# Places of the projections' operands in memory, and a last norm without a second spread

## The chip, the cores and the metric

The kernel runs on one core of a Trainium2 chip. The metric is the device time of one execution in microseconds, median over several runs. Five engines work side by side and wait for one another through semaphores: PE (TensorE, matrix products into PSUM), ACT (ScalarE), DVE (VectorE), POOL (GpSimd) and SP (SyncE, which here issues most DMAs). On-chip memory (SBUF) has 128 partitions; a tile occupies the same bytes in each of them. PE reads its operands from SBUF and writes to PSUM.

## The reference

One inference step of a small encoder trunk, float32, width 2048, for 256 frames of a new stream and 32 frames of a running one. The kernel puts both side by side: T = 288 columns. With `rmsnorm(x, g) = x * rsqrt(mean(x*x) + 1e-6) * g`:

```python
for l in range(2):
    h = rmsnorm(x, norm_mix_g[l])
    mix = ab_mixer(h) if l == 0 else c_mixer(h)   # retention and GLA heads; band attention
    x = x + mix                                   # both end in a projection 2048 -> 2048
    h = rmsnorm(x, norm_ffn_g[l])
    g, u = split(h @ w_up)                        # 2048 -> 2 * 5632
    act = silu(conv3(g) + b) * u
    x = x + act @ w_down                          # 5632 -> 2048
y = rmsnorm(x, norm_final_g)
```

States of the heads, keys and values and the last rows of the convolution are outputs too. All weights are float32 and each is used once.

## The kernel before

Everything lies with features on partitions: a tile [128, 288] holds 128 features of all tokens, and x is 16 of them. A projection makes one output tile [128, 288] in a PSUM bank by summing over k-tiles of 128 input features (`project`, lines 61 to 74). A float32 product is made of float32r ones (rounded operands, which PE takes in one pass): each operand is split into a rounded part and the rest, h and l, and three products are summed, h·xh, h·xl and l·xh (`passes`, lines 77 to 81). So each k-tile costs three matmuls of 288 columns, each with its own load of 128 x 128 weights.

Weights come in tiles of up to 8 k-tiles (`weights`, lines 50 to 59): SP issues the DMA into w (4 buffers), ACT casts it into wh, DVE makes wl (3 buffers each). The moving operands are of two kinds. xh and xl, 16 tiles each, hold the split x with a norm's gain (`gain_in`, lines 135 to 141); they feed the input projection, q, k, v and the FFN's up projections, and the norm's factor R is multiplied in behind them. bh and bl hold what goes into output and down projections: 16 tiles each in a pool of their own, and for the FFN six more, bh16 to bh21 and bl16 to bl21, which `ffn` takes from its pool. The FFN is done in two halves of 22 hidden tiles: 22 pairs of up projections, then 16 down projections over the 22 k-tiles of that half, added to x.

The order of each engine's work is the order in which the program issues it; a tile framework adds the waits. Tiles of a pool lie one behind another in the order in which they are first asked for, each rounded up to 32 bytes, and a pool opened later begins where the one before ends. The first pool, "const", holds xh0 to xh15, xl0 to xl15, R, ones, gains and ident in this order; then come the pools of the weights, of small tiles, and the rest.

Norms: while x[m] becomes final, ACT squares it and DVE adds the squares into ssq (`square_in`). `norm_stat` (from line 156) sums ssq over partitions with the tokens as outputs (9 or 18 matmuls of one column), takes the inverse root of 3 columns on 96 partitions, and spreads it again: DVE scales an identity by it, PE multiplies that by all ones, ACT copies the result to R, [128, 288]. At the end of the last FFN the last square goes into a tile of its own (sq_last) and is a second summand. Then y = x * R, with the gain already in x but for the last tile: 11 products on DVE and 5 on POOL, stored in four DMAs of 2, 4, 5 and 5 tiles, all issued by SP.

Of the kernel before, what the change touches and what calls it, by code (L numbers as in the profile page):

```python
# [33 lines left out]
class Trunk:  # L34
# [15 lines left out]
    def weights(self, src, n, lo=False):  # L50
        """n k-tiles of 128 rows: the float32 tile as the sum of two float32r tiles."""
        nc = self.nc
        w = self.wp.tile([P, WCH, P], F32, name="w", tag="w", bufs=4)[:, :n, :]
        h = self.wp.tile([P, WCH, P], F32R, name="wh", tag="wh", bufs=3)[:, :n, :]
        l = self.wp.tile([P, WCH, P], F32R, name="wl", tag="wl", bufs=3)[:, :n, :]
        nc.sync.dma_start(w, src)
        nc.scalar.copy(h, w)  # L57
        nc.vector.tensor_tensor(l, w, h.bitcast(F32), op=ALU.subtract)  # L58
        return h, l

    def project(self, src, xh, xl, nk, k0=0, chunks=None, part=None, ps=None):
        """PSUM [128 outputs, T]: the product over nk k-tiles of float32 operands split in two."""
        if ps is None:
# [19 lines left out]
    def first_project(self, src, x):  # L83
        """As project, while the input is loaded and the first norm's operands come about."""
        nc = self.nc
# [13 lines left out]
    def first_squares(self, x):  # L99
        """The sum of squares, in the place of x."""  # L100
        nc, sq = self.nc, x
        for c in range(0, KD, 4):
            nc.scalar.activation(sq[:, c : c + 4, :], x[:, c : c + 4, :], AF.Square)
            if c:
                nc.vector.tensor_tensor(sq[:, 0:4, :], sq[:, 0:4, :], sq[:, c : c + 4, :], op=ALU.add)
        nc.vector.tensor_tensor(sq[:, 0:2, :], sq[:, 0:2, :], sq[:, 2:4, :], op=ALU.add)
        nc.vector.tensor_tensor(sq[:, 0, :], sq[:, 0, :], sq[:, 1, :], op=ALU.add)
        self.ssq = sq[:, 0, :]
# [8 lines left out]
    def rsqrt(self, out, ms_ps, inv_n, p=P, n=T, tag="rs"):  # L117
        """out = (ms_ps * inv_n + eps) ** -0.5"""
        nc = self.nc
# [10 lines left out]
    def norm_in(self, k, n):  # L130
        """x[k] is final: its split product with the gain of norm n, and its square."""
        self.gain_in(k, n)
# [23 lines left out]
    def norm_stat(self):  # L156
        """R [128, T]: each token's 1 / rms, on all partitions; worked out with tokens on partitions."""
        nc = self.nc
# [21 lines left out]
    def run(self, ctx):  # L180
# [5 lines left out]
        nc.vector.memset(self.ones, 1.0)  # L186
        self.gains = self.const("gains", [P, 5, KD], F32, a["gains"], nc.scalar)
        self.sq_last = None
# [7 lines left out]
        with self.tc.tile_pool(name="x", bufs=1) as xp:  # L196
# [5 lines left out]
            with self.tc.tile_pool(name="f0", bufs=2) as pool:  # L202
                self.ffn(pool, 0, 2)
            with self.tc.tile_pool(name="c", bufs=2) as pool:
# [5 lines left out]
            with self.tc.tile_pool(name="f1", bufs=2) as pool:  # L210
                self.ffn(pool, 1, 4)

    def chain(self, heads, front, tail):
        """Heads as generators of steps. A head's steps after its first few take turns with the next one's
        first, so that its later products find their operands ready."""
        for _ in range(front):
# [9 lines left out]
    def out_start(self, w, chunks):  # L226
        """The first halves of out_proj's first sums, which the last head is not part of."""
        self.started = [self.project(w[m], self.bh, self.bl, KD, chunks=chunks, part=0) for m in range(2)]

    def start(self, pool):  # L230
        """The first norm, and the layer's first products beside it."""
        nc, a = self.nc, self.a
# [4 lines left out]
        k0 = self.first_project(w[KB], x_in)  # L237
        # The gate's low-rank features: both parts of the weights side by side in one tile's columns
        # (their sum is taken in the product with w2, which stands twice).
        lo_ps = self.acc_ps.tile([P, 512], F32, name="acc", tag="acc")[:, :T]  # L240
# [18 lines left out]
    def out_proj(self, w, n, chunks):  # L259
        """x += o @ w, and the next norm's start."""  # L260
        for m in range(KD):
# [7 lines left out]

    def ffn(self, pool, layer, n):  # L270
        nc, a = self.nc, self.a
        convp = self._one(pool, "convp", [P, NF, 4], a["convp"][:, layer])
        hist = self._one(pool, "hist", [P, NF, 2], a["hist"][:, layer])
        conv_out = self._one(pool, "conv_out", [P, NF, 4])
        gps = [self._one(pool, f"gp{i}", [P, T + 4]) for i in range(3)]
        for gp in gps:
            nc.gpsimd.memset(gp[:, 0:2], 0.0)
        bh = self.bh + [self._one(pool, f"bh{k}", [P, T], None, F32R) for k in range(KD, HALF)]
        bl = self.bl + [self._one(pool, f"bl{k}", [P, T], None, F32R) for k in range(KD, HALF)]
        up, down = a["w_ffn_up"][layer], a["w_ffn_down"][layer]  # L280
        last = layer == 1
        for half in range(2):
# [29 lines left out]
            for m in range(KD):  # L312
                ps = self.project(down[m], bh, bl, HALF, half * HALF)
                nc.vector.tensor_tensor(self.x[m], self.x[m], ps, op=ALU.add)
                if half == 1:
                    if last:
                        self.square_in(m, m == KD - 1)
                        if m < KD - 1:
                            nc.scalar.activation(self.x[m], self.x[m], AF.Copy, scale=self.gains[:, n, m : m + 1])
                    else:  # L320
                        self.norm_in(m, n)
        self.norm_stat()
        if last:
            y = pool.tile([P, KD, T], F32, name="y", tag="y", bufs=1)
            cuts = (0, 2, 6, 11, 16)
            for i, j in zip(cuts, cuts[1:]):
                for k in range(i, j):
                    if k == KD - 1:
                        nc.vector.scalar_tensor_tensor(
                            y[:, k, :], self.x[k], self.gains[:, n, k : k + 1], self.R, op0=ALU.mult, op1=ALU.mult  # L330
                        )
                        continue
                    eng = nc.gpsimd if k % 3 == 1 else nc.vector
                    eng.tensor_tensor(y[:, k, :], self.x[k], self.R, op=ALU.mult)  # L334
                nc.sync.dma_start(a["yT"][:, i:j, :], y[:, i:j, :])

# [1 line left out]

# [5 lines left out]
    def head_out(self, pool, o, gates, hd, g):  # L344
        """Gated, normalised head output into the split operands of w_out; o: two PSUM tiles."""
        nc = self.nc
# [17 lines left out]
    def to_tokens(self, pool, feats, name, width, scale=None, bufs=1):  # L364
        """[128 tokens, 3, width] from feature-major [128, T] tiles."""
        nc = self.nc
# [21 lines left out]
    def ab_mixer(self, pool, k0, q0, lo_ps):  # L388
# [19 lines left out]
        def gates():  # L408
            """log sigmoid of the gates, tokens on partitions (its 1/16 is in the level matrices)."""
            e = pool.tile([P, 9, T], F32, name="E", tag="E").rearrange("p l t -> p (l t)")  # L410
# [38 lines left out]
    def gla_head(self, pool, hd, w, la, lvl, masks, eyem, hg, first):  # L449
# [13 lines left out]

        # E[:, l]: decays to and from the middle of each token's block of level l. Slot 7: level 256
        # (tile 0 before, tile 1 behind the middle), and from the sample's start; slot 8: to the end.
        E = pool.tile([P, 9, T], F32, name="E", tag="E", bufs=1)
# [29 lines left out]

        # Scores, transposed: each pair of tokens belongs to the one level whose middle parts them.
        pT = [pool.tile([P, T - t * P], F32, name=f"pT{t}", tag=f"pT{t}") for t in range(2)]
# [64 lines left out]

        # States.
        kf = pool.tile([P, T], F32, name="kf", tag="kf", bufs=1)
# [86 lines left out]

# [1 line left out]

    def att_head(self, pool, hd):
# [7 lines left out]
        nc.gpsimd.dma_start(vc, a["cache_v"][hd])  # L663
        # Keys stand in reversed order: the bias of query p and key column c is rel[c0 + p + c].
        bias = pool.tile([P, TP], F32, name="bias", tag="bias")
# [19 lines left out]
        nc.tensor.matmul(pss[:, TS:T], lhsT=q[:, TP:], rhs=kc, start=True, stop=True)  # L685
        # Tokens on partitions: the sample's, then the prompt's second and first 128.
        vt = pool.tile([P, 3, P], F32, name="avt", tag="avt")
# [25 lines left out]
        yield  # L713
        # Probabilities with keys on partitions: the first 128 and the second of the prompt's
        # (p0, p1), beside them the cache's two halves, and the sample's own (p2).
        p0 = pool.tile([P, T], F32, name="ap0", tag="ap0")
# [25 lines left out]
def _tiles(w):  # L742
    """[K, M] -> [M/128, 128, K/128, 128]: one output tile's rows, contiguous by partition."""
    k, m = w.shape
# [3 lines left out]
def _cols(v):  # L748
    """[..., N] -> [128, ..., N/128]: features on partitions."""
    v = v.reshape(*v.shape[:-1], v.shape[-1] // P, P)  # L750
# [110 lines left out]
```

## Time and profile before

| | us |
|---|---|
| median of 3 runs | 2762.46 (2761.59 to 2763.56) |
| the profiled execution, span from first to last instruction | 2760.1 |
| PE busy | 2732.1 |
| DVE busy | 1572.3 |
| ACT busy | 1123.9 |
| POOL busy | 126.5 |

The profile is of one execution on the one core; its own time is the span of 2760.1 us, and the timed runs hold some 2 us more around it. The page gives busy time by engine, the chain of work that ended last (at each step back to what released it), and groups of instructions by line, engine and operation with count, busy time, mean length, idle time before and what ended that. "x694: 292/294/294, 1004.8 to 1279.7" in a row of one line's instructions is their count, shortest, median and longest length in ns, and the starts of the first and the last in us.

### The profile page before, as it was taken

The page shows a single profiled execution, that of the slowest core. Times are in us where ns is not written, and L with a number is a line of the kernel's source. Part 1 is how long each engine was busy: PE and PEld are TensorE (multiplying, and loading weights), DVE is VectorE, ACT ScalarE, POOL GpSimd, SP SyncE. Part 2 cuts the span into 40 slices and gives each one's busy share as a digit, 9 for nine tenths or more (in the row PEclk, how much of TensorE's full clock was granted, in tenths as well). Part 3 has the DMA queues.
Part 4 walks back from the last instruction along what each step waited for, and adds up shares of the span by engine and source line. Part 5 has one row for each costly group of instructions (what it writes and reads, how often), then busy time and mean ns, then how long its engine had stood idle before and what let it go on. Part 6 is the DMA issues. An engine that isn't in the chain of part 4 may idle for free.

```text
span 2760.1 us, 49198 instructions
## 1 busy us (share of the span) xinstructions
PE 2732.1 (99%) x20340; PEld 2686.5 (97%) x20340; DVE 1572.3 (57%) x2536; ACT 1123.9 (41%) x1538; POOL 126.5 (5%) x440
## 2 busy tenths in 40 slices
PE   8999999999999999999999999999999999999997
PEld 7999999999999999999999999999999999999997
DVE  6566555666665456665555555556666544666544
ACT  7444343443343333334444333344333333433443
POOL 1000000000000000000011111100000000000000
PEclk9999999999999999999999999999999999999999
DMA  5334444545555555555555555544555555555553
GB/s 198 117 131 142 152 157 149 192 162 166 168 167 161 168 168 165 167 168 162 166 182 170 166 165 165 163 156 162 166 165 166 162 167 168 168 166 166 163 167 125
DMA packets 126546, 448.84 MB, mean 163 GB/s; under 512 B 15562, under 2 KB 15754, under 8 KB 126320
## 3 DMA queue, kind: packets, MB, share of 16 engines
q1 hardware_dynamic: 119520, 427.15, 48.6%
q0 software_dynamic: 6656, 18.49, 2.1%
q8 instruction: 159, 2.61, 0.4%
q14 instruction: 67, 0.55, 0.1%
q10 hardware_dynamic: 144, 0.04, 0.0%
HBM read 435.22 MB, written 10.40 MB: 161 GB/s over the span
## 4 chain that ended last, share of the span: by engine, by line
PE 97%; ACT 1%; DVE 1%; DMA 1%; issue 0%; SPq 0%; DVEq 0%; ACTq 0%
PE acc L80 31%; PE acc L79 30%; PE acc L81 30%; PE mm L520 1%; DMA x_in<-in_xT 0%; PE mm L372 0%; PE mm L643 0%; ACT wh L57 0%; PE mm L682 0%; PE mm L685 0%; PE mm L734 0%; PE mm L681 0%; DVE wl L58 0%; DVE y L334 0%; PE mm L738 0%
## 5 line engine op out<-in xcount | busy, mean ns | idle before, releaser
L57 ACT CAST wh<-w 128x1024 fp32r<-128x1024 f32 (+1 forms) x816 | 843.7, 1034 | 1505.9 <-PE acc L80 1209.0
L58 DVE TENSOR_TENSOR wl<-w,wh 128x1024 fp32r<-128x1024 f32 (+1 forms) x816 | 981.0, 1203 | 761.7 <-ACT wh L57 761.4
L79 PE MATMUL acc<-xh,wh 128*128 128x288 f32 x4480 | 1323.0, 295 | 8.6 <-ACT wh L57 7.7
L81 PE MATMUL acc<-xh,wl 128*128 128x288 f32 x4480 | 1323.5, 295 | 1.3 <-DVE wl L58 1.3
L80 PE MATMUL acc<-xl,wh 128*128 128x288 f32 x4480 | 1324.0, 296 | 0.0
L79 PEld LDWEIGHTS acc<-xh,wh 128*128 128x128 f32 x4480 | 843.2, 188 | 13.3 <-ACT wh L57 7.9
L81 PEld LDWEIGHTS acc<-xh,wl 128*128 128x128 f32 x4480 | 842.6, 188 | 2.8 <-DVE wl L58 2.1
L80 PEld LDWEIGHTS acc<-xl,wh 128*128 128x128 f32 x4480 | 843.0, 188 | 2.0 <-issue 1.0
L79 PE MATMUL acc<-bh,wh 128*128 128x288 f32 x1920 | 567.1, 296 | 0.4 <-ACT wh L57 0.4
L80 PE MATMUL acc<-bl,wh 128*128 128x288 f32 x1920 | 566.3, 295 | 0.0
L81 PE MATMUL acc<-bh,wl 128*128 128x288 f32 x1920 | 565.0, 294 | 0.0
L79 PEld LDWEIGHTS acc<-bh,wh 128*128 128x128 f32 x1920 | 360.1, 188 | 1.3 <-ACT wh L57 0.6
L81 PEld LDWEIGHTS acc<-bh,wl 128*128 128x128 f32 x1920 | 361.2, 188 | 0.0
L80 PEld LDWEIGHTS acc<-bl,wh 128*128 128x128 f32 x1920 | 360.3, 188 | 0.1
L298 DVE SCALAR_TENSOR_TENSOR gc<-gp,convp,gc 128x290 f32<-128x290 f32 x176 | 91.3, 519 | 3.2
L304 DVE TENSOR_TENSOR v<-acc,R 128x288 f32<-128x288 f32 x88 | 40.3, 458 | 87.8 <-PE acc L81 87.8
L289 DVE TENSOR_TENSOR gp<-acc,R 128x256 f32<-128x256 f32 x88 | 37.5, 426 | 88.3 <-PE acc L81 88.3
L291 POOL COPY conv_out<-gp 128x2 f32<-128x2 f32 x88 | 16.4, 187 | 1312.7 <-DVE gp L289 1312.7
L114 ACT CAST bh<-v 128x288 fp32r<-128x288 f32 x88 | 38.1, 433 | 15.3 <-DVE v L306 15.3
L296 DVE TENSOR_SCALAR gc<-gp,convp 128x290 f32<-128x290 f32 x88 | 38.0, 432 | 9.5
L305 DVE TENSOR_TENSOR v<-v,sg 128x256 f32<-128x256 f32 x88 | 37.5, 426 | 9.9 <-DVE v L304 0.9
L115 DVE TENSOR_TENSOR bl<-v,bh 128x288 fp32r<-128x288 f32 x88 | 39.8, 452 | 0.7 <-ACT bh L114 0.7
(256 smaller groups left out, 1188.2 us busy)
## 6 DMA issues: line engine op xcount, KB each, us to landing
w<-in_w_ffn_up SPq DMA_DIRECT2D x352, 512.0 KB, 3.7
w<-in_w_ffn_down SPq DMA_DIRECT2D x128, 512.0 KB, 3.7
w<-in_w_in SPq DMA_DIRECT2D x112, 512.0 KB, 3.8
w<-in_w_qkv SPq DMA_DIRECT2D x96, 512.0 KB, 3.9
w<-in_w_ffn_down SPq DMA_DIRECT2D x64, 384.0 KB, 3.2
w<-in_w_out_ab SPq DMA_DIRECT2D x32, 512.0 KB, 3.8
w<-in_w_out_att SPq DMA_DIRECT2D x32, 512.0 KB, 3.8
x<-in_xT SPq DMA_DIRECT2D x4, 576.0 KB, 6.1
```

The lines of the kernel that those rows point to most:

```text
L57: nc.scalar.copy(h, w)
L58: nc.vector.tensor_tensor(l, w, h.bitcast(F32), op=ALU.subtract)
L79: nc.tensor.matmul(ps, lhsT=h, rhs=xh, start=first, stop=False)
L80: nc.tensor.matmul(ps, lhsT=h, rhs=xl, start=False, stop=False)
L81: nc.tensor.matmul(ps, lhsT=l, rhs=xh, start=False, stop=last)
L114: self.nc.scalar.copy(h, v)
L115: self.nc.vector.tensor_tensor(l, v, h.bitcast(F32), op=ALU.subtract)
L289: nc.vector.tensor_tensor(gp[:, 2 : TP + 2], g[:, :TP], self.R[:, :TP], op=ALU.mult)
L296: nc.vector.tensor_scalar(gc, gp[:, 0:W], cw[:, 0:1], cw[:, 3:4], op0=ALU.mult, op1=ALU.add)
L298: nc.vector.scalar_tensor_tensor(gc, gp[:, w : w + W], cw[:, w : w + 1], gc, op0=ALU.mult, op1=ALU.add)
L304: nc.vector.tensor_tensor(v, u, self.R, op=ALU.mult)
L305: nc.vector.tensor_tensor(v[:, :TP], v[:, :TP], s[:, :TP], op=ALU.mult)
```

## The change

Four edits; the comments that the diff also drops are left out.

- The tile of the gains is asked for with 96 columns (384 bytes a partition) in place of 80 (320 bytes); its DMA is issued apart, as before by ACT, into the first 80.
- In `ffn`, bh16 to bh21 and bl16 to bl21 are asked for ahead of the pool's other tiles. `ffn` also takes a [128, 1] tile eps and has POOL fill it.
- In the last FFN the gain is multiplied into x[15] on ACT as well, behind its square.
- `norm_stat` is not called at the end. `out_norm` takes its place: all ones times ssq and all ones times sq_last put the sum on all partitions at once, [128, 288] in PSUM; ACT takes the square root from PSUM (scale 1/D, eps as bias), DVE makes v = sum/D + eps beside it, then the reciprocal and one Newton step, on all 288 columns. Then four products of four tiles each on DVE, with r broadcast over the four, each stored by its own DMA, issued in turn by SP and ACT.

```diff
@@ run
-        self.gains = self.const("gains", [P, 5, KD], F32, a["gains"], nc.scalar)
+        gains = self.const("gains", [P, 96])[:, : 5 * KD].rearrange("p (n k) -> p n k", n=5)
+        nc.scalar.dma_start(gains, a["gains"])
+        self.gains = gains
...
-                self.ffn(pool, 0, 2)
+                self.ffn(pool, 0, 2, x)
...
-                self.ffn(pool, 1, 4)
+                self.ffn(pool, 1, 4, x)
@@ ffn
-    def ffn(self, pool, layer, n):
+    def ffn(self, pool, layer, n, x_all):
         nc, a = self.nc, self.a
+        bh = self.bh + [self._one(pool, f"bh{k}", [P, T], None, F32R) for k in range(KD, HALF)]
+        bl = self.bl + [self._one(pool, f"bl{k}", [P, T], None, F32R) for k in range(KD, HALF)]
         convp = self._one(pool, "convp", [P, NF, 4], a["convp"][:, layer])
...
-        bh = self.bh + [self._one(pool, f"bh{k}", [P, T], None, F32R) for k in range(KD, HALF)]
-        bl = self.bl + [self._one(pool, f"bl{k}", [P, T], None, F32R) for k in range(KD, HALF)]
+        eps = self._one(pool, "eps", [P, 1])
+        nc.gpsimd.memset(eps, EPS)
...
                         self.square_in(m, m == KD - 1)
-                        if m < KD - 1:
-                            nc.scalar.activation(self.x[m], self.x[m], AF.Copy, scale=self.gains[:, n, m : m + 1])
+                        nc.scalar.activation(self.x[m], self.x[m], AF.Copy, scale=self.gains[:, n, m : m + 1])
                     else:
                         self.norm_in(m, n)
-        self.norm_stat()
         if last:
-            y = pool.tile([P, KD, T], F32, name="y", tag="y", bufs=1)
-            cuts = (0, 2, 6, 11, 16)
-            for i, j in zip(cuts, cuts[1:]):
-                for k in range(i, j):
-                    if k == KD - 1:
-                        nc.vector.scalar_tensor_tensor(
-                            y[:, k, :], self.x[k], self.gains[:, n, k : k + 1], self.R, op0=ALU.mult, op1=ALU.mult
-                        )
-                        continue
-                    eng = nc.gpsimd if k % 3 == 1 else nc.vector
-                    eng.tensor_tensor(y[:, k, :], self.x[k], self.R, op=ALU.mult)
-                nc.sync.dma_start(a["yT"][:, i:j, :], y[:, i:j, :])
+            self.out_norm(pool, x_all, eps)
+        else:
+            self.norm_stat()
+
+    def out_norm(self, pool, x, eps):
+        nc = self.nc
+        ps = self.mm()[:, :T]
+        nc.tensor.matmul(ps, lhsT=self.ones, rhs=self.ssq, start=True, stop=False)
+        nc.tensor.matmul(ps, lhsT=self.ones, rhs=self.sq_last, start=False, stop=True)
+        v = pool.tile([P, T], F32, name="fv", tag="fv", bufs=1)
+        r = pool.tile([P, T], F32, name="fr", tag="fr", bufs=1)
+        s = pool.tile([P, T], F32, name="fs", tag="fs", bufs=1)
+        nc.scalar.activation(r, ps, AF.Sqrt, bias=eps, scale=1.0 / D)
+        nc.vector.tensor_scalar(v, ps, 1.0 / D, EPS, op0=ALU.mult, op1=ALU.add)
+        nc.vector.reciprocal(r, r)
+        nc.vector.tensor_tensor(s, r, r, op=ALU.mult)
+        nc.vector.scalar_tensor_tensor(s, s, -0.5, v, op0=ALU.mult, op1=ALU.mult)
+        nc.vector.scalar_tensor_tensor(r, s, 1.5, r, op0=ALU.add, op1=ALU.mult)
+        y = pool.tile([P, KD, T], F32, name="y", tag="y", bufs=1)
+        for n, i in enumerate(range(0, KD, 4)):
+            c = slice(i, i + 4)
+            nc.vector.tensor_tensor(y[:, c, :], x[:, c, :], r[:, None, :].to_broadcast([P, 4, T]), op=ALU.mult)
+            (nc.scalar if n % 2 else nc.sync).dma_start(self.a["yT"][:, c, :], y[:, c, :])
```

## The prediction

> **What bounds the kernel now.** First the page: its busy shares, its chain of work that ended last, and its groups.
>
> ```profile
> span 2760.1 us, 49198 instructions
> ...
> PE 2732.1 (99%) x20340; PEld 2686.5 (97%) x20340; DVE 1572.3 (57%) x2536; ACT 1123.9 (41%) x1538; POOL 126.5 (5%) x440
> ...
> PEclk9999999999999999999999999999999999999999
> ...
> PE 97%; ACT 1%; DVE 1%; DMA 1%; issue 0%; SPq 0%; DVEq 0%; ACTq 0%
> ...
> L57 ACT CAST wh<-w 128x1024 fp32r<-128x1024 f32 (+1 forms) x816 | 843.7, 1034 | 1505.9 <-PE acc L80 1209.0
> ...
> L79 PE MATMUL acc<-xh,wh 128*128 128x288 f32 x4480 | 1323.0, 295 | 8.6 <-ACT wh L57 7.7
> ...
> L79 PE MATMUL acc<-bh,wh 128*128 128x288 f32 x1920 | 567.1, 296 | 0.4 <-ACT wh L57 0.4
> ```
>
> PE holds 97% of the chain at a full clock. It waits 8.6 us for weights in the whole run, while the cast of the weights waits 1209 us for PE: weights lie ready, and DMA, ACT and DVE are cover. So the time is the number of projection matmuls, (4480 + 1920) x 3 = 19200, by their step, plus the tail behind the last one. The mean of 295 ns is a pipelined length; the step comes from first and last starts. These are the rows of line 79 (one matmul of three in a k-tile) in four stretches: up projection, the two output projections, down projection.
>
> ```profile
> L79 PE MATMUL acc<-xh,wh x694: 292/294/294, 1004.8 to 1279.7; 128*128 128x288 f32 x174
> L79 PE MATMUL acc<-bh,wh x175: 295/295/297, 510.0 to 579.6; 128*128 128x288 f32 x175
> L79 PE MATMUL acc<-bh,wh x213: 295/295/297, 1809.8 to 1894.6; 128*128 128x288 f32 x107
> L79 PE MATMUL acc<-bh,wh x326: 288/295/298, 870.1 to 999.7; 128*128 128x288 f32 x163
> ```
>
> Up: 274.9 / 693 = 0.3967 us a k-tile, 132.2 ns a matmul. Output projections: 69.6 / 174 and 84.8 / 212, both 0.4000, 133.3 ns. Down: 129.6 / 325 = 0.3988, 132.9 ns. The operations are the same; what differs is where the moving operand lies. In the built program xh0 starts at byte 16512 of its partition (129 x 128) and each such tile is 1152 bytes (9 x 128), so xh and xl all start on a multiple of 128. The 320 bytes of the gains (2.5 x 128) then shift what is allocated behind them: w, wh, wl and bh0 to bh15, bl0 to bl15 stand 64 bytes past one. The small tiles of the FFN pool (convp to gp2, 5312 bytes, 41.5 x 128) shift bh16 to bh21 back onto one. The down projection thus holds the comparison inside one output: k-tiles 0 to 15 from shifted operands, 16 to 21 from unshifted ones. Its timeline, PE alone (start, length):
>
> ```profile
> 2700.34 0.29 PE L79 MATMUL acc<-bh,wh 128*128 128x288 f32 x1
> ...
> 2705.54 0.30 PE L79 MATMUL acc<-bh,wh 128*128 128x288 f32 x1
> ...
> 2705.94 0.29 PE L79 MATMUL acc<-bh,wh 128*128 128x288 f32 x1
> ...
> 2708.32 0.30 PE L79 MATMUL acc<-bh,wh 128*128 128x288 f32 x1
> ```
>
> 13 k-tiles in 5.20 us are 0.4000; the last six, from 2705.94 to the next output at 2708.32, take 2.38, 0.3967. The step changes where the operand's place changes, with the same weight buffers. A read of 1152 bytes from +64 touches ten blocks of 128 bytes, from 0 nine; the extra one would cost 1.11 ns a matmul.
>
> **The change, part one: places.** Gains take 384 bytes, and the FFN's bh16 to bl21 come first in their pool. All of wh, wl, bh, bl, xh, xl then start on multiples of 128. No instruction is added but one POOL memset for eps at each FFN's start; POOL waits at that place anyway and nothing reads eps before the end:
>
> ```profile
> L288 POOL COPY gp<-hist 128x2 f32<-128x2 f32 x88 | 17.6, 203 | 212.8 <-DVE gc L298 205.3 <-DMA hist<-in_hist 7.5
> ```
>
> If that cover were gone it would cost some 0.2 us twice. The gains' DMA stays one on ACT's queue; nothing else there moves.
>
> The moving operand: output projections 2 x 16 x 16 = 512 k-tiles x (0.4000 - 0.3967) = 1.7 us; down projections 2 x 2 x 16 x 22 = 1408 k-tiles x (0.3988 - 0.3967) = 2.9 us. Together **-4.6 us**; starts are given to 0.1 us, which leaves this between 4.0 and 5.3. The xh matmuls keep their step.
>
> The stationary operand: no row of the projections shows unshifted weights. The only weights of this size on a multiple of 128 are the all-ones tile:
>
> ```profile
> L353 PEld LDWEIGHTS mm<-hsq,ones x16: 187/188/189, 89.7 to 486.2; 128*128 128x128 f32 x16
> ...
> L79 PEld LDWEIGHTS acc<-xh,wh x694: 188/188/188, 1005.1 to 1280.0; 128*128 128x128 f32 x174
> ```
>
> Load times are alike, and a load runs beside the matmul before it, so I take 0. The bounds: 512 bytes from +64 touch five blocks, not four; at 1.11 ns each, 19200 x 1.11 = 21.3 us of gain on one side, and a loss of the same step on the other (rival A).
>
> [...]
>
> **Part two: the tail.** Before, from the last projection's sum on, every engine:
>
> ```profile
> 2743.61 0.46 DVE L314 TENSOR_TENSOR x<-x,acc 128x288 f32<-128x288 f32 x1 [6.71 <-PE acc L81]
> 2744.10 0.44 ACT L147 ACTIVATE sql<-x 128x288 f32<-128x288 f32 x1 [7.65 <-DVE x L314]
> ...
> 2744.59 0.33 PE L164 MATMUL mm<-ones,sql 128*96 128x1 f32 x2 [0.94 <-ACT sql L147]
> ...
> 2745.64 0.16 DVE L123 TENSOR_SCALAR rv<-mm 96x3 f32<-96x3 f32 x1 [1.58 <-PE mm L164]
> ...
> 2748.12 0.40 ACT L178 COPY R<-mm 128x288 f32<-128x288 f32 x1 [2.08 <-PE mm L175]
> 2748.55 6.75 DVE L334 TENSOR_TENSOR y<-x,R 128x288 f32<-128x288 f32 x10 [1.07 <-ACT R L178]
> 2748.60 4.91 POOL L334 TENSOR_TENSOR y<-x,R 128x288 f32<-128x288 f32 x5 [150.00 <-ACT R L178]
> ...
> 2755.22 0.51 DVE L329 SCALAR_TENSOR_TENSOR y<-x,gains,R 128x288 f32<-128x288 f32 x1
> ```
>
> Sum and square stay; the new all-ones product with the last square starts at 2744.59 too. (The one with ssq runs while DVE and ACT work on x; the added gain of x[15] follows the square on ACT.) The durations for what comes next:
>
> ```profile
> L353 PE MATMUL mm<-hsq,ones 128*128 128x288 f32 x16 | 5.2, 405 | 0.0
> ...
> L319 ACT ACTIVATE x<-x,gains 128x288 f32<-128x288 f32 x15 | 8.1, 539 | 0.5
> ...
> L124 ACT ACTIVATE rsq<-rv 128x288 f32<-128x288 f32 x8 | 3.6, 445 | 0.1
> ...
> L125 DVE RECIPROCAL ry<-rsq 128x288 f32<-128x288 f32 x8 | 15.6, 1949 | 2.1 <-ACT rsq L124 2.1
> ...
> L105 DVE TENSOR_TENSOR x_in<-x_in 128x1152 f32<-128x1152 f32 x3 | 4.1, 1356 | 1.1 <-ACT x_in L103 1.1
> L128 DVE SCALAR_TENSOR_TENSOR hr<-rsq,ry 128x288 f32<-128x288 f32 x8 | 3.6, 455 | 0.1
> ...
> L127 DVE SCALAR_TENSOR_TENSOR rsq<-rsq,rv 128x288 f32<-128x288 f32 x8 | 3.6, 453 | 0.1
> L126 DVE TENSOR_TENSOR rsq<-ry 128x288 f32<-128x288 f32 x8 | 3.6, 449 | 0.0
> ```
>
> A float32 product is two instructions: 5.2 / 8 = 0.65 us, so PSUM is ready at 2745.24, 0.4 before the old 2745.64. ACT is free by then (2744.54 + 0.54 = 2745.08). Then, with 0.04 between steps as in the timeline: square root 0.445 (v on DVE beside it), reciprocal 1.949, 0.449, 0.453, 0.455, in all 3.75 + 0.24: the products start near 2749.20, **0.65 later** than the old 2748.55. Wide rows cost more than the 3-column ones, and that eats what the removed second spread by PE and the copy gave.
>
> The products: four of 1152 elements at 1.356 with gaps make 5.5, to 2754.7, against 2755.73 before, where DVE's 288-column products took (6.75 + 0.51) / 11 = 0.66 each beside POOL's. **1.0 earlier.** L105 has no broadcast operand; four single products by the 0.449 row would be 1.80, so up to 1.8 more in all. The square root reads PSUM while v does: 0 to 0.45 more. I take L105 and 0, having the same sizes and engines.
>
> The last store:
>
> ```profile
> L335 SPq DMA_DIRECT2D out_yT<-y x4: 332/338/348, 2749.7 to 2755.8; - x4
> ...
> DMA to landing us min/median/max: 2.1/2.9/3.3
> ...
> out_yT<-y SPq DMA_DIRECT2D x2, 720.0 KB, 3.2
> ...
> gains<-in_gains ACTq DMA_DIRECT2D x1, 40.0 KB, 3.3
> ...
> out_yT<-y SPq DMA_DIRECT2D x1, 576.0 KB, 2.8
> ```
>
> Before: issued at 2755.8, landed 3.3 later at 2759.1, 1.0 before the span's end. After: 576 KB, not 720, issued at 2754.8, 2.8: 2757.6. It goes by ACT's queue, for which only the gains' 3.3 stands: 0.5 more or less. Nothing is queued behind it. Between 288 KB at 2.1 and 720 KB at 3.3 lie 1.2 us, so 576 KB move in some 1.6 us and come every 1.36: the last may wait up to 0.7. I take 2.8. **Tail -1.5 us**; the bounds are -2.0 and, with all that could be added (1.8 + 0.45 + 0.5 + 0.7), +1.9.
>
> **Sum.** -4.6 - 1.5 = -6.1. The profiled execution is its span, 2760.1, which becomes 2754.0; the median of the timed runs lies 2.4 above that span, so **2756.3** against 2762.46. Own range 2754.5 to 2759.5. 0.2%, about what a measurement here can tell from no change, is 5.5 us.
>
> **Rivals.**
>
> A, slower: not the count of blocks but equal places make the slow step. Every slow matmul has moving and stationary operand both at +64, every fast one has 0 against +64; none here has both at 0. If two reads at the same place within 128 bytes collide, the change makes every pair collide: 13440 xh matmuls x 1.11 = +14.9, the 2 x 2 x 16 x 6 x 3 = 1152 of k-tiles 16 to 21 +1.3, the rest stays, tail -1.5: 2777. It decides as soon as unshifted pairs step at 133.3. For it: the trace can't part the two. Against: it needs two reads to meet where the count needs one. [...]
>
> B, the places do nothing: the step of bh follows from something that stays, say the order of its buffers; only the tail moves, 2761.0. Against: the step turns at k-tile 16, in the middle of a sum. A new weight tile begins there too, but the one that begins at k-tile 8 turns nothing. [...]
>
> C, weights count too: each load saves up to 1.11 ns, 2756.3 - 21.3 = 2735 at the full price. Against: the load times of 188 ns at either place, and that loads are hidden.
>
> **How the numbers follow.** Forecast 0.62, A 0.12, B 0.14, C 0.12. The range 2742 to 2762.5 takes the forecast with its unknown tail, B, and C up to two thirds of its price; it leaves A out. Faster by over 0.2% (below 2756.9): 0.7 of the forecast's 0.62, since its centre lies only 0.6 inside, and C: 0.55. Within: the rest of the forecast and B, 0.33. Slower: A, 0.12.
>
> **What would show it.** Line 79 at 0.3967 a k-tile in output and down projections, without a turn at k-tile 16, and the same in the up projection. Products from 5.6 us behind the last sum's start, each 1.36; last store 2.8 to landing. A shows as 0.400 in the up projection, B as 0.400 in the output projections, C as less than 0.3967 everywhere. It is wrong if the tail's broadcast products or ACT's store are slow, or if PE begins to wait for weights.

## The result and the profile after

The changed kernel takes **2776.37 us** (2776.15 to 2777.43, 5 runs) beside 2761.77 for the kernel before: ratio 1.0049, 95% interval 1.0038 to 1.0060. It is slower, by nearly what rival A had priced (2777), and the forecast of 2756.3 was wrong in sign.

The page of the profile after, lines that answer to those shown of before:

```profile
span 2774.3 us, 49152 instructions
...
PE 2747.5 (99%) x20326; PEld 2701.2 (97%) x20326; DVE 1572.2 (57%) x2526; ACT 1123.3 (40%) x1538; POOL 121.5 (4%) x437
...
PEclk9999999999999999999999999999999999999999
...
PE 97%; ACT 1%; DMA 1%; DVE 1%; issue 0%; SPq 0%; DVEq 0%; ACTq 0%
...
L57 ACT CAST wh<-w 128x1024 fp32r<-128x1024 f32 (+1 forms) x816 | 842.0, 1032 | 1523.2 <-PE acc L80 1223.8
...
L79 PE MATMUL acc<-xh,wh 128*128 128x288 f32 x4480 | 1333.8, 298 | 7.7 <-ACT wh L57 7.6
...
L79 PEld LDWEIGHTS acc<-xh,wh 128*128 128x128 f32 x4480 | 840.6, 188 | 12.4 <-ACT wh L57 7.8
```

PE is busy 15.4 us longer at the same granted clock (0.998 in both), still holds 97% of the chain, and still hardly waits for weights (7.7 us in the row shown, 8.6 before), while the casts wait for PE as before (1223.8 us, 1209.0 before). So no new wait and no other engine took the time: the matmuls themselves step more slowly. The rows of line 79 in an up projection, an output projection and a down projection (count, lengths in ns, first and last start):

```profile
L79 PE MATMUL acc<-xh,wh x688: 288/295/297, 1009.8 to 1284.6; 128*128 128x288 f32 x172
L79 PE MATMUL acc<-bh,wh x176: 295/296/297, 1834.8 to 1904.8; 128*128 128x288 f32 x176
L79 PE MATMUL acc<-bh,wh x330: 295/296/297, 873.0 to 1004.6; 128*128 128x288 f32 x165
```

274.8 / 687, 70.0 / 175 and 131.6 / 329 are all 0.4000 us a k-tile, 133.3 ns a matmul. Before, the up projection had 0.3967, the output projections 0.4000, the down projections 0.3988. With all operands on multiples of 128, every stage has the *slow* step. The last projection matmul starts at 2758.16 in the timeline after (below), and before at 2743.28:

```profile
2743.28 0.29 PE L81 MATMUL acc<-bh,wl 128*128 128x288 f32 x1
```

It is 14.9 us late. The tail then gives 0.7 back (from that start to the end of the span 16.8 before, 16.1 after), which makes the 14.2 between the spans.

The tail's timeline after, from the last sum on (start, length):

```profile
2758.16 0.29 PE L81 MATMUL acc<-bh,wl 128*128 128x288 f32 x1
...
2758.49 0.46 DVE L319 TENSOR_TENSOR x<-x,acc 128x288 f32<-128x288 f32 x1 [6.74 <-PE acc L81]
2758.98 0.44 ACT L147 ACTIVATE sql<-x 128x288 f32<-128x288 f32 x1 [7.67 <-DVE x L319]
...
2759.48 0.75 PE L336 MATMUL mm<-sql,ones 128*128 128x288 f32 x2 [0.54 <-ACT sql L147]
2760.33 0.50 ACT L340 ACTIVATE fr<-mm,eps 128x288 f32<-128x288 f32 x1 [0.34 <-PE mm L336]
2760.86 0.46 DVE L341 TENSOR_SCALAR fv<-mm 128x288 f32<-128x288 f32 x1 [1.91 <-ACT fr L340]
2761.24 1.94 DVE L342 RECIPROCAL fr<-fr 128x288 f32<-128x288 f32 x1
...
2764.69 5.17 DVE L349 TENSOR_TENSOR y<-x,fr 128x1152 f32<-128x1152 f32 x4
```

The products begin 6.2 us behind the start of the last sum. The line of v (fv) shows one reason: v does not run beside the square root but waits for its end, and the reciprocal stands behind v on DVE.

### The profile page after: what moved, and what is told of

It reads as the page before. It is cut to its first block, busy times and chain, and to the rows that moved or that the text cites. A ratio compares the mean times of both kernels' runs of the same rounds, so it can differ in the third digit from the quotient of the medians.

```text
span 2774.3 us, 49152 instructions
## 1 busy us (share of the span) xinstructions
PE 2747.5 (99%) x20326; PEld 2701.2 (97%) x20326; DVE 1572.2 (57%) x2526; ACT 1123.3 (40%) x1538; POOL 121.5 (4%) x437
## 4 chain that ended last, share of the span: by engine, by line
PE 97%; ACT 1%; DMA 1%; DVE 1%; issue 0%; SPq 0%; DVEq 0%; ACTq 0%
PE acc L79 31%; PE acc L81 30%; PE acc L80 30%; PE mm L535 1%; DMA x_in<-in_xT 0%; PE mm L387 0%; PE mm L658 0%; PE mm L697 0%; PE mm L700 0%; PE mm L749 0%; PE mm L696 0%; ACT wh L57 0%; PE mm L753 0%; ACT L492 0%; PE mm L659 0%
## 5 line engine op out<-in xcount | busy, mean ns | idle before, releaser
L57 ACT CAST wh<-w 128x1024 fp32r<-128x1024 f32 (+1 forms) x816 | 842.0, 1032 | 1523.2 <-PE acc L80 1223.8
L80 PE MATMUL acc<-xl,wh 128*128 128x288 f32 x4480 | 1324.1, 296 | 0.0
L81 PE MATMUL acc<-xh,wl 128*128 128x288 f32 x4480 | 1320.8, 295 | 1.2 <-DVE wl L58 1.1
L81 PEld LDWEIGHTS acc<-xh,wl 128*128 128x128 f32 x4480 | 844.4, 188 | 2.8 <-DVE wl L58 2.0
L80 PEld LDWEIGHTS acc<-xl,wh 128*128 128x128 f32 x4480 | 842.0, 188 | 2.0 <-issue 1.0
L80 PE MATMUL acc<-bl,wh 128*128 128x288 f32 x1920 | 566.3, 295 | 0.0
L81 PE MATMUL acc<-bh,wl 128*128 128x288 f32 x1920 | 564.2, 294 | 0.0
L81 PEld LDWEIGHTS acc<-bh,wl 128*128 128x128 f32 x1920 | 361.6, 188 | 0.0
L80 PEld LDWEIGHTS acc<-bl,wh 128*128 128x128 f32 x1920 | 360.3, 188 | 0.1
L114 ACT CAST bh<-v 128x288 fp32r<-128x288 f32 x88 | 38.2, 434 | 15.4 <-DVE v L311 15.4
L319 DVE TENSOR_TENSOR x<-x,acc 128x288 f32<-128x288 f32 x64 | 29.1, 454 | 20.1 <-PE acc L81 20.1
```

What stands on the lines that cost most here:

```text
L80: nc.tensor.matmul(ps, lhsT=h, rhs=xl, start=False, stop=False)
L81: nc.tensor.matmul(ps, lhsT=l, rhs=xh, start=False, stop=last)
L114: self.nc.scalar.copy(h, v)
```

## The experiments

### Which operand's place?

Two kernels that undo the coincidence from opposite sides. In the first, wh and wl are slices of wider tiles, 64 bytes on; everything else is the kernel after.

```diff
+    def padded(self, name, off):
+        t = self.wp.tile([P, WCH * P + 32], F32R, name=name, tag=name, bufs=3)
+        return t[:, off // 4 : off // 4 + WCH * P].rearrange("p (k m) -> p k m", k=WCH)
...
-        h = self.wp.tile([P, WCH, P], F32R, name="wh", tag="wh", bufs=3)[:, :n, :]
-        l = self.wp.tile([P, WCH, P], F32R, name="wl", tag="wl", bufs=3)[:, :n, :]
+        h = self.padded("wh", 64)[:, :n, :]
+        l = self.padded("wl", 64)[:, :n, :]
```

> The kernel after, with wh and wl moved 64 bytes on, all moving operands left on multiples of 128. Equal places (a matmul steps at 133.3 ns where moving and stationary operand lie at the same place within 128 bytes, at 132.2 where they lie 64 apart): 0.3967 us a k-tile in all stages, the 19200 matmuls of the slow step give back 1.0 to 1.1 ns each, 2755.5 to 2757 us. Unshifted weights (the weights' own place makes the slow step, wherever the moving operand lies): the same. Neither (something else of the new layout, the source tiles w on multiples of 128 for instance): 2776.

In the second, weights stay on multiples of 128, and 64 bytes of padding stand ahead of xh and ahead of bh; another 64 behind xl put the weights back in their place.

```diff
+        self.const("pad0", [P, 16])
         self.xh = [self.const(f"xh{k}", [P, T], F32R) for k in range(KD)]
         self.xl = [self.const(f"xl{k}", [P, T], F32R) for k in range(KD)]
+        self.const("pad1", [P, 16])
...
+        bp.tile([P, 16], F32, name="pad2", tag="pad2")
         self.bh = [bp.tile([P, T], F32R, name=f"bh{k}", tag=f"bh{k}") for k in range(KD)]
```

> The kernel after, with xh, xl, bh and bl moved 64 bytes on, weights left on multiples of 128. Equal places: 0.3967 everywhere, 2755.5 to 2757 us, like the run with the weights moved. Unshifted weights: 0.400 everywhere, 2776. Blocks of the moving operand, the count of the prediction: ten blocks a read, no faster than 0.400, 2776 or more.

Measured: weights moved **2753.56 us** (ratio to before 0.9968, 0.9956 to 0.9980); moving operands moved **2756.50** (0.9979, 0.9970 to 0.9987). Line 79's matmul (line 83 in the first kernel) in an up and a down projection, first of the kernel with the weights moved, then of the one with the moving operands moved:

```profile
L83 PE MATMUL acc<-xh,wh x670: 290/294/300, 1010.0 to 1274.8; 128*128 128x288 f32 x168
...
L83 PE MATMUL acc<-bh,wh x328: 290/294/300, 870.0 to 999.7; 128*128 128x288 f32 x164
```

```profile
L79 PE MATMUL acc<-xh,wh x669: 292/293/294, 1009.9 to 1274.9; 128*128 128x288 f32 x168
...
L79 PE MATMUL acc<-bh,wh x328: 292/294/294, 869.9 to 999.6; 128*128 128x288 f32 x164
```

0.3958 and 0.3966; 0.3966 and 0.3966 us a k-tile. The second kernel came within the expected 2755.5 to 2757; the first came 1.9 us below, since its up projections step a little faster than the rule of equal places says. Its weight buffers lie 4224 bytes apart, the second kernel's 4096; the two versions with the weights at 112, below, show that the distance counts (131.3 ns a matmul in up and 131.8 in down projections at 4224, 131.1 in both at 4608).

With all moving operands 64 bytes *past* a multiple of 128, the place that the prediction had charged with a tenth block, the step is the fast one. That ends the count of blocks. It ends "unshifted weights are slow" too, since the weights lie unshifted there. And the place of w, the source tile, is not it: the first kernel leaves w where the changed kernel has it. What the slow rows share is the difference: 0 between the places of the two operands within 128 bytes (133.3 ns a matmul, against 131.9 to 132.2 in these two kernels). So rival A's rule holds in the four combinations of 0 and 64 that now exist. That two reads collide in memory is the author's reading; no row shows the collision itself.

### The tail alone

The kernel before with the new last norm: gains as a [P, 5, KD] tile again, bh16 to bl21 behind the small tiles again.

> The kernel before, all places as there, with the new last norm alone. From the trace of the changed kernel, where the last sum's start to the end of the span is 15.8 us against 16.5: 0.7 us faster than before, 2761.1. By the prediction's sum 1.5 faster, 2760.3. If the tail were slower as it stands in this layout, above 2761.8.

Measured: 2761.22 beside 2762.91, ratio 0.9995 (0.9986 to 1.0004). By time alone the tail can't be told from nothing, nor the 0.7 from the 1.5. Its trace has the tail of the kernel after, with products of 1.35 us and the same idle time of 1.9 us ahead of v:

```profile
L349 DVE TENSOR_TENSOR y<-x,fr x4: 1349/1350/1358, 2751.0 to 2754.8; 128x1152 f32<-128x1152 f32 x4
...
  DVE fv L341: 1.9, 1
```

So 0.7 us, read from traces, is what the new tail saves. With the places of before, the new tail costs nothing: the change's slowdown is all in the places.

### How the step depends on the place

The first sweep lets the place of wh and wl change from stage to stage; the moving operands stay on multiples of 128. Each sweep was run once, and the steps are read inside that execution. A place below is that of the weights, in bytes past a multiple of 128.

```diff
-        h = self.wp.tile([P, WCH, P], F32R, name="wh", tag="wh", bufs=3)[:, :n, :]
+        h = self.padded("wh", self.off)[:, :n, :]
...
         for half in range(2):
+            self.off = ((32, 96), (16, 112))[layer][half]
...
+            self.off = ((48, 80), (4, 60))[layer][half]
             for m in range(KD):
                 ps = self.project(down[m], bh, bl, HALF, half * HALF)
```

> The kernel after with the place of wh and wl changed from stage to stage, moving operands on multiples of 128. Bytes past a multiple of 128: input projection 0, first output projection 64, first FFN's up projections 32 and 96 (its halves), down 48 and 80, q, k and v 64, second output projection 8, last FFN's up 16 and 112, down 4 and 60. Equal places as a collision of two reads with a coarse grain of 64 bytes: 0.400 a k-tile for 0 to 60, 0.3967 from 64 on. With a fine grain: 0.400 at 0 alone (and 4, 8), 0.3967 elsewhere. A gradual dependence: steps between these, lowest at 64. If only 64 of the tried places is fast, the alignment to 64 matters beside the difference.

Up projections: 132.4 ns a matmul at 32, 133.7 at 96, 133.1 at 16, 131.3 at 112. None of the grains expected (coarse, fine, a valley at 64) holds: 112 beats 64, and 96 beside it is worse than 0. Its down projections (48, 80, 4, 60) all lie between 132.7 and 132.9. Two more sweeps repeat and extend it with weight buffers of 4608 bytes, a multiple of 512, where the first had 4224; wh and wl get a place each (against the kernel after):

```diff
+    def padded(self, name, i):
+        t = self.wp.tile([P, WCH * P + 128], F32R, name=name, tag=name, bufs=3)
+        off = self.off[i] // 4
+        return t[:, off : off + WCH * P].rearrange("p (k m) -> p k m", k=WCH)
```

> The places of the run before this one again in other stages, with all weight buffers at the same place within 512 bytes (there they stood 4224 bytes apart). Bytes past a multiple of 128: input projection 16, first output projection 48, layer 0 first half 64, second half 112, q, k and v 0, second output projection 80, layer 1 first half 96, second half 32. If the place within 128 bytes sets the step: as there, 131.3 ns a matmul at 112 (lowest), 132.0 at 64, 132.4 at 32, 133.1 at 16, 133.3 at 0, 133.7 at 96 (highest), the same in up and down projections. If the place within 256 or 512 bytes or the buffers' distance counts: other values, and up and down apart.

> Places beyond 128 bytes, weight buffers all at the same place within 512. Layer 0 first half: up 128, down 240; second half: up 192, down 368; layer 1 first half: up 256, down 496; second half: up 320, down 120; q, k and v 448; input projection 176; output projections 104 and 124. If the place within 128 bytes sets the step: 133.3 ns at 128 and 256, 132.0 at 192, 320 and 448, 131.3 at 240, 368 and 496. If a longer period counts: these groups fall apart.

Line 79's matmul (line 84 there), of the second sweep: up at 64, up and down at 112, up and down at 96, up at 32.

```profile
L84 PE MATMUL acc<-xh,wh x606: 292/293/295, 619.8 to 859.8; 128*128 128x288 f32 x152
...
L84 PE MATMUL acc<-xh,wh x675: 292/293/294, 1009.7 to 1274.8; 128*128 128x288 f32 x169
...
L84 PE MATMUL acc<-bh,wh x331: 292/293/294, 1285.1 to 1414.9; 128*128 128x288 f32 x166
...
L84 PE MATMUL acc<-xh,wh x625: 293/295/298, 1930.1 to 2179.7; 128*128 128x288 f32 x157
...
L84 PE MATMUL acc<-bh,wh x336: 293/296/298, 2184.9 to 2320.0; 128*128 128x288 f32 x168
...
L84 PE MATMUL acc<-xh,wh x681: 292/298/299, 2330.0 to 2599.7; 128*128 128x288 f32 x171
```

Of the third: up at 128, down at 240, up at 192, down at 368 and 496.

```profile
L84 PE MATMUL acc<-xh,wh x600: 295/296/297, 620.0 to 859.6; 128*128 128x288 f32 x150
...
L84 PE MATMUL acc<-bh,wh x331: 292/293/293, 870.0 to 999.8; 128*128 128x288 f32 x166
...
L84 PE MATMUL acc<-xh,wh x681: 292/293/294, 1010.0 to 1279.8; 128*128 128x288 f32 x171
...
L84 PE MATMUL acc<-bh,wh x331: 292/293/293, 1290.0 to 1419.8; 128*128 128x288 f32 x166
...
L84 PE MATMUL acc<-bh,wh x331: 292/293/293, 2190.0 to 2319.8; 128*128 128x288 f32 x166
```

Last start less first start, over the count less one, over three: 0 (the kernel after), 128 and 256 give 133.3 ns; 64, 192 and 320 give 132.2; 112, 240, 368 and 496 give 131.1. So the mean of a stage repeats every 128 bytes, as far as these places go.

A single k-tile does not. The moving tiles are 1152 bytes long, 9 x 128, so from one k-tile to the next they lie alternately on an odd and an even multiple of 128, while the weights, 512 bytes a k-tile in buffers 4608 = 18 x 256 apart, keep their place within 256. A mean over a stage can't tell a period of 256 from one of 128. The starts in the traces, to the ns, can. The length of a k-tile, by the place of its weights less that of its moving tiles, within 256 bytes (from the addresses in the built programs):

| down projections | ns a k-tile, two differences |
|---|---|
| third sweep at 240, at 368 and at 496 | 389.1 to 389.2 at 112; 397.4 to 397.5 at 240 |
| second sweep at 96 | 400.0 at 96; 406.7 at 224 |
| moving operands at 64 (second kernel above) | 396.7 at 64; 396.7 at 192 |
| the changed kernel | 400.0 at 0; 400.0 at 128 |

At 240 and at 496 the even k-tiles are the short ones, at 368, where the weights lie 128 bytes further on within 256, the odd ones. So 131.1 ns is the mean of k-tiles of 389 and 397.5 ns, and the length of a single k-tile has a period of 256 bytes at least.

A finer sweep, with the same buffers:

> Finer places, buffers 4608 apart. Input projection 24, output projections 40 and 20, layer 0 first half up 116, down 108; second half up 108, down 104; q, k and v 100; layer 1 first half up 44, down 56; second half up 52, down 48. [...] If it is a smooth valley around 112 and 48: 131 to 131.5 at 108, 116 and 52. Up and down at 108 the same, if the kind of moving operand does not count.

Mean ns a matmul, by the place of the weights within 128 bytes, moving operands on multiples of 128, buffers 4608 apart, of stages of projections alone (two values are of different stages):

| place | step | | place | step |
|---|---|---|---|---|
| 0 | 133.3 | | 64 | 132.2 |
| 20 | 135.6 | | 80 | 133.3 |
| 32 | 132.2 | | 96 | 133.3 up, 134.4 down |
| 40 | 132.2 | | 104 | 133.3 |
| 44 | 134.5 | | 108 | 132.7 and 132.8 |
| 48 | 131.1 output, 133.3 down | | 112 | 131.1 |
| 52 | 132.2 | | 116 | 132.2 |
| 56 | 132.4 | | 120 | 132.2 |
| | | | 124 | 133.3 |

The dependence is no smooth valley (131.1 at 112, 132.2 four bytes on, 133.3 at 104). Nor do multiples of 16 bytes stand apart: 104 and 40, which are none, step at 133.3 and 132.2 like 80 and 32, which are, and 0, 64 and 112 have three steps (133.3, 132.2 and 131.1). Most values sit 1.1 ns apart: 131.1, 132.2, 133.3, 134.4. At least two of these are means of two lengths of k-tile: 131.1 (389 and 397.5) and the 134.4 at 96 (400.0 and 406.7). At 48 and 96 the same place gives two values in different stages, so the place within 128 bytes is not all. The place within 256 is part of the rest, but not all of it: the up projections at 96 have 401.0 and 399.0 at the same two differences. What else counts stays open.

In all these sweeps only the weights were moved. That the difference of the two places decides, and not the weights' own place, was tried with both operands for 0 and 64 alone; the swap of the short k-tiles between 240 and 368 speaks for it at 112, as far as steps of 128 bytes go.

### A version from the best place

wh and wl at 112 in every stage, buffers first 4224, then 4608 bytes apart.

```diff
-        h = self.wp.tile([P, WCH, P], F32R, name="wh", tag="wh", bufs=3)[:, :n, :]
-        l = self.wp.tile([P, WCH, P], F32R, name="wl", tag="wl", bufs=3)[:, :n, :]
+        h = self.padded("wh", 112)[:, :n, :]
+        l = self.padded("wl", 112)[:, :n, :]
```

> The kernel after with wh and wl 112 bytes past a multiple of 128 in every stage. If the 131.3 ns of the one stage hold everywhere: 0.75 ns less than with 64 on 19200 matmuls, some 14 us below the 2753.6 of that run, 2739. If they were that stage's alone (its buffers, its moving operand): 2750 to 2756.

Measured: 2742.41 us, ratio 0.9926 (0.9909 to 0.9942); somewhat above 2739, since its output and down projections step at 131.7 to 131.8 where its up projections have 131.3.

> The kernel after with wh and wl 112 bytes past a multiple of 128 and their buffers 4608 bytes apart (36 times 128, nine times 512) where the run before had 4224. If the place within 512 bytes and the even distance make the 131.12 ns of the three stages seen: 0.2 ns less on 13440 matmuls and 0.7 on 5760, some 6 us below that run's 2742.4, so 2735 to 2738. If the buffers' distance does nothing: 2742.

Measured: **2737.84 us**, ratio 0.9909 (0.9895 to 0.9924), within what was expected. The same matmul in its up and down projections:

```profile
L83 PE MATMUL acc<-xh,wh x675: 292/293/293, 1004.8 to 1269.9; 128*128 128x288 f32 x169
...
L83 PE MATMUL acc<-bh,wh x332: 292/293/293, 864.7 to 994.9; 128*128 128x288 f32 x166
```

265.1 / 674 and 130.2 / 331: 0.3933 in both. The version beats both kernels: 0.9% below the one before, with no instruction of the projections changed. From the changed kernel's 133.3 ns to 131.1 on 19200 matmuls would be 42 us; the medians, of two sets of runs, lie 38.5 apart.

### Which load meets which read?

A weight load runs beside the matmul ahead of it: in the timeline of the kernel after, a load of L81 and the matmul of L80 ahead of it both start at 2756.83. If the pair that counts is a matmul and the *next* one's load, xh meets wh, xl meets wl, xh meets the next wh; if it is a matmul and the weights it uses, the pairs are xh with wh, xl with wh, xh with wl. To part them, xl and bl were moved against xh and bh and the two weight tiles against each other.

```diff
+    def padded(self, name, i):
+        t = self.wp.tile([P, WCH * P + 32], F32R, name=name, tag=name, bufs=3)
+        off = self.off[i] // 4
+        return t[:, off : off + WCH * P].rearrange("p (k m) -> p k m", k=WCH)
...
+        h = self.padded("wh", 0)[:, :n, :]
+        l = self.padded("wl", 1)[:, :n, :]
...
+        self.const("pad0", [P, 16])
         self.xl = [self.const(f"xl{k}", [P, T], F32R) for k in range(KD)]
...
+            self.off = (((64, 0), (0, 64)), ((64, 64), (0, 0)))[layer][half]
             for fl in range(HALF):
```

> Which load meets which read. The kernel after, with xl and bl moved 64 bytes on, xh and bh at 0, and wh and wl placed apart, changing from stage to stage. Both FFNs: layer 0 first half (up and down) wh 64, wl 0; second half wh 0, wl 64; layer 1 first half both 64, second half both 0. The load beside it (a matmul is slowed by the load of the weights of the next one, which runs beside it): the three of a k-tile run beside loads of wh, wl, wh; so layer 0 first half meets no equal places, 132.2 ns a matmul, second half three of three, 133.3; layer 1 first half one of three (xl beside wl), 132.6, second half two of three, 132.95. Its own weights (the place of the weights already in the array): layer 0 first half two of three, 132.95, second half one of three, 132.6; layer 1 as in the other theory, one and two of three. No difference of the halves of layer 0 would speak against both.

Up projections in the order of the expectation (layer 0 first and second half, layer 1 first and second): 132.4, 132.7, 132.7, 132.6 ns. The halves of layer 0 differ in the direction of the load beside it, but by 0.3 where 1.1 was expected: inconclusive. It was done again with xl and bl moved by 32 and buffers 4608 apart.

> Which load meets which read, again, with buffers 4608 apart, so that only the place within 128 bytes counts. xh and bh at 0, xl and bl at 32. Places of wh and wl: input projection, layer 0 first half, q, k, v: 112 and 16; output projections and layer 0 second half: 112 and 112; layer 1 first half: 0 and 16; second half: 112 and 0. Steps by difference as measured: 131.12 at 112, 133.33 at 0 and 80, 133.3 to 134.4 at 96, 132.76 at 16. The load beside it (the pairs are xh with wh, xl with wl, xh with wh): layer 0 first half 112 three times, 131.12 ns a matmul; second half 131.9; layer 1 first half 132.6; second half 131.9 to 132.2. Its own weights (xh with wh, xl with wh, xh with wl): layer 0 first half 132.4, second half 131.9; layer 1 first half 133.1 to 133.5, second half 132.6.

Its up projections: layer 0 first half, second half, layer 1 first half, second half.

```profile
L84 PE MATMUL acc<-xh,wh x603: 292/294/298, 619.9 to 859.7; 128*128 128x288 f32 x151
...
L84 PE MATMUL acc<-xh,wh x681: 293/293/294, 1010.1 to 1279.8; 128*128 128x288 f32 x171
...
L84 PE MATMUL acc<-xh,wh x630: 288/295/298, 1929.9 to 2179.9; 128*128 128x288 f32 x158
...
L84 PE MATMUL acc<-xh,wh x684: 294/294/295, 2330.1 to 2599.9; 128*128 128x288 f32 x171
```

132.8, 132.2, 132.5, 131.7. The first half of layer 0 should have had 131.1 by the load beside it and has 132.8, so that theory falls as stated; its own weights, 132.4 there, miss layer 1 (133.1 to 133.5 and 132.6 expected, 132.5 and 131.7 measured). Under neither pairing are the steps of mixed places the mean of the steps of their pairs. The step put in for 112 was itself a mean of two lengths of k-tile, which weakens the test. Which load meets which read stays open.

### The tail's missing gain

v made by ACT behind its square root, on top of the best version; v is there without the added 1e-6.

```diff
-        nc.vector.tensor_scalar(v, ps, 1.0 / D, EPS, op0=ALU.mult, op1=ALU.add)
+        nc.scalar.activation(v, ps, AF.Copy, scale=1.0 / D)
```

> The kernel of the run with even buffers and 112 bytes, with v (mean square, here without the added 1e-6) made by ACT behind its square root, so that DVE has nothing ahead of the reciprocal. If the tail's missing gain sits in DVE waiting with v for ACT's square root over the same PSUM tile: the reciprocal starts 0.35 to 0.4 us earlier behind the last sum, the products 5.8 us behind its start where it was 6.2, the whole 2737.4. If the reciprocal is held by something else, the products stay at 6.2.

The tail's timeline before this edit, and with it:

```profile
2720.27 0.45 DVE L323 TENSOR_TENSOR x<-x,acc 128x288 f32<-128x288 f32 x1 [6.59 <-PE acc L85]
...
2723.01 1.94 DVE L346 RECIPROCAL fr<-fr 128x288 f32<-128x288 f32 x1
...
2726.47 5.16 DVE L353 TENSOR_TENSOR y<-x,fr 128x1152 f32<-128x1152 f32 x4
```

```profile
2718.92 0.46 DVE L323 TENSOR_TENSOR x<-x,acc 128x288 f32<-128x288 f32 x1 [6.59 <-PE acc L85]
...
2721.15 0.40 ACT L345 ACTIVATE fv<-mm 128x288 f32<-128x288 f32 x1
2721.29 1.95 DVE L346 RECIPROCAL fr<-fr 128x288 f32<-128x288 f32 x1 [1.91 <-ACT fr L344]
...
2724.83 5.16 DVE L353 TENSOR_TENSOR y<-x,fr 128x1152 f32<-128x1152 f32 x4
```

The reciprocal comes 2.37 us behind the sum's start in place of 2.74, the products 5.91 in place of 6.20. So the wait of v, with v itself, was 0.3 to 0.4 us of the tail, a little less than expected (products at 5.8). The time is 2736.15, ratio 0.9903 (0.9887 to 0.9920); against the version without this edit (0.9909) the intervals overlap.

## Why the prediction was wrong

**What bounds the kernel: right.** PE's step times 19200 is what moved, with the same 97% of the chain, the same clock (0.998), and a wait for weights that went from 8.6 to 7.7 us.

**The steps of before: right numbers, wrong reading.** 0.3967, 0.4000 and 0.3988, and the turn at k-tile 16, are all there. But in every row of before the weights stood at +64. A comparison in which one operand moves and the other stands still can't tell "where the moving operand lies" from "where it lies relative to the weights". The prediction read the first and priced a tenth block at 1.11 ns; the kernel with all moving operands at +64 and the step at 0.3966 shows that no such price exists.

**The step that failed** is thus "the xh matmuls keep their step", with the 0 taken for the stationary operand under it. The price for it was in the text as a bound, "a loss of the same step on the other" side. The evidence taken for the 0, load times of 187 to 189 ns at either place, speaks of the length of a load, and not of what the load does to the matmul beside it: the loads of the kernel after are 188 ns too. The measured term: 4480 k-tiles x 3.33 ns = 14.9 us more, where 0 stood. The second term, -4.6 for output and down projections, became 1408 x (0.4000 - 0.3988) = +1.7: the k-tiles 16 to 21, that had been fast, became slow, and the rest stayed. Together 16.6 against the 14.9 by which the last projection matmul starts late; the input and the q, k, v stretches, where other products stand between, rose by 1.9 and 2.0 us where the full step would give 3.0 and 2.6.

**Rival A** had this with its place, its price and its decisive sign (0.400 in the up projection), and 2777 against the measured 2776.4. That it came so close is in part luck: its 16.2 for the places (14.9 measured) and its -1.5 for the tail (-0.7) err against each other. Its chance of 0.12 was too low by the prediction's own words: nothing in the trace parted it from the forecast. What was held against it, that it needs two reads to meet, was no observation. **B** falls with it, **C** as well: weights at multiples of 128 saved nothing. Yet C's size was not absurd: a better place of the weights is worth more than 21 us (2737.84 is 25 below the 2762.90 of the kernel before in the same set of runs), only not by the number of blocks.

**The tail: right sign, half the size**, -0.7 against -1.5. The start of the all-ones product (0.99 behind the sum's start), the reciprocal (1.94 against 1.949) and the broadcast products (1.35 against 1.356) came as read from their rows; the four take 5.17 in all, 0.3 less than the 5.5 of the sum. Mis-sized: the product 0.75 us, not 0.65; the square root 0.50, not 0.445; v behind it, 0.4, the bound "0 to 0.45" that was set to 0 and came nearly whole; together the products start 0.6 late. And the stores, two of them on ACT's queue, the last among these:

```profile
L350 ACTq DMA_DIRECT2D out_yT<-y x2: 338/342/347, 2767.3 to 2769.9; - x2
...
DMA to landing us min/median/max: 2.8/3.2/3.4
```

The time to landing grows from store to store (2.8, 3.1, 3.3, 3.4), and the last, issued at 2769.9, takes the 3.4, where the sum took 2.8. That is 0.6 more, within the 0.7 that the prediction allowed for a store that waits for the one ahead. From its landing to the span's end it is 1.0, as before.

## What to carry to other kernels

Where a difference between two places in one kernel is read as the effect of one operand, ask which other operand stood still in every row; if one did, the relative reading has the same evidence, and needs the same chance. When TensorE's step bounds a kernel, the bytes by which its two SBUF operands stand apart can be tried as a size of its own: here 0, 64 and 112 bytes gave 133.3, 132.2 and 131.1 ns a matmul, and padding wh and wl was worth 0.9%. Aligning everything to one round number makes all operands coincide, which was among the slower places here, though not the slowest (133.3 ns at 0, 135.6 at 20, 134.5 at 44). And before a mean is read as a rule with a period, look at the single steps: here two lengths alternated under it.

## What the runs showed of the hardware

- A float32r matmul of 288 columns with its 128 x 128 load steps at a mean of 131.1, 132.2, 133.3 or 134.4 ns in most stages, by the places of its operands: for 0 and 64 by their difference, elsewhere with the weights alone moved. The mean repeats every 128 bytes (0 = 128 = 256; 64 = 192 = 320; 112 = 240 = 368 = 496). Single places gave 135.6 (20) and 134.5 (44).
- The single k-tile of three such matmuls does not repeat every 128 bytes: with the weights 112 bytes past the moving tile it takes 389 ns, with 240 bytes 397.5.
- The distance of the weight buffers counts too: at 112, 4224 bytes apart gave 131.3 in up and 131.8 in down projections, 4608 apart 131.1 in both.
- A VectorE instruction that reads the PSUM tile which ScalarE is reading began only behind it (idle 1.91 us, released by the square root). In the built program that instruction waits for a semaphore of ScalarE, so the wait is the program's own; whether the chip would let both read at once was not tried.
